# Where the low halves of a product's operands are made: a subtraction on VectorE, or a negated copy on ScalarE and an adding transfer

## The chip, the cores and the metric

One core of a Trainium2 chip runs the whole kernel in one launch. The metric is the device time of one execution in microseconds, the median over runs. TensorE does the matrix products, VectorE (DVE), ScalarE (ACT) and GpSimd (POOL) the elementwise work, and transfers are issued by SyncE (SP) and GpSimd.

## The reference

One layer of a decoder trunk with 512 tokens of 1024 channels, in float32. Two gated token mixers (a convolution and a chunked linear attention) are merged and projected; then comes the channel mixer, which the change touches, and a last normalization:

```python
merged = jax.nn.sigmoid(gate_a) * y_conv + jax.nn.sigmoid(gate_b) * y_gla
h = h + merged @ w_o[l]

u2 = _rmsnorm(h, norm2_g[l])
z = _causal_dwconv(u2 @ w_ffn_up[l], ffn_dw_w[l], ffn_dw_b[l])      # 2 x 2816 channels, width 3
h = h + (jax.nn.silu(z[..., :FFN_DIM]) * z[..., FFN_DIM:]) @ w_ffn_down[l]
...
return _rmsnorm(h, final_g)
```

## The kernel before

A float32 product is made of three TensorE products of a rounded format (float32r). Each operand x is split in a high part, hi = x rounded, and a low part, lo = x - hi; `mm3` (lines 448 to 450) then issues low times high, high times low, and high times high into the same accumulator. The left operand of a matmul is loaded as the weights, the right one streams by. So each operand needs a rounding copy (on ScalarE) and a subtraction (on VectorE), and a matmul can't start before both parts of both operands are there. For weights, `split_weight` does it (lines 355 and 356, and 385 and 390); for the sixteen weight tiles in `ADDED`, line 387 writes the negated copy with ScalarE and line 388 adds the weight to it by a transfer from off-chip memory that GpSimd issues.

The channel mixer has 22 tiles of 128 channels. They are handled in pairs, and the pairs in three groups of four, three and four (`GROUPS`). For each group the up products of its tiles come first, in an order that `up_plan` gives; the up products are `col_tile` for single tiles and `two_tiles` for two at once, whose summed weights GpSimd makes (line 327). A tile's two accumulators are convolved (lines 1500 and 1503), passed through silu (1511) and multiplied (1517). The result of the first tile of a pair is `w`, that of the second is `f`. When a group's up products are done, `seven("w_down", ...)` makes the group's part of the down product for 1024 output channels, and adds it to the residual `hres` (line 1419).

`seven` does a product of two by two blocks by seven block products instead of eight. For each pair of tiles, it needs seven left operands: blocks of `w` and `f`, and sums of such blocks. They are made in three steps, each of them ending in `fsplit`, which makes the high and the low part of one tile:

- `first_of_pair`: `w` gets a third block (line 1533); tile y (`yh`, `yl`, 512 columns) holds the operands named a11 and n3.
- `second_of_pair`: tile a (`ah`, `al`, 512 columns) holds a12 and a22, from `f`.
- `second_of_pair`, further on: three sums of blocks into `v` (lines 1543 to 1545); tile s (`sh`, `sl`, 768 columns) holds s1, n2 and s4.

With 11 pairs, that is 33 calls of `fsplit`. The split tiles have four buffers each; `w`, `f` and `v` have one. The products within `seven` go by steps: a11 for the pairs first, then a12, s1 and the others, each with two pairs at a time, so TensorE reads yl first, then al, then sl. For the down weights, `sum_on` (line 317) and the line 300 add further blocks of the weight to a loaded one by transfers that GpSimd issues.

The order of the instructions on each engine is that of the recording, changed by a scheduler; transfers and weight sums that are kept in program order, and constraints of the form "issue after", hold it in places. Transfers that GpSimd issues go to one queue, and a place on GpSimd's instruction stream comes when all before it have been issued.

Of the kernel before, what the change touches and what calls it, by code (L numbers as in the profile page):

```python
# [10 lines left out]
F32 = mybir.dt.float32  # L11
# [4 lines left out]
ALU = mybir.AluOpType  # L16
# [3 lines left out]
T = 512  # L20
# [55 lines left out]
def trunk_layer(ctx: ExitStack, tc: tile.TileContext, a: dict, out: bass.AP):  # L76
    nc = tc.nc
# [23 lines left out]
    def nm(s):  # L101
        return f"{s}_{next(names)}"

    def heap(dt=F32):
        return hp.tile([P, T], dt, tag="h", name=nm("h"))
# [710 lines left out]
    for k in range(KT):  # L816
# [4 lines left out]
        c = heap()  # L821
# [108 lines left out]
    for k in range(KT):  # L930
        s = slice(k * P, (k + 1) * P)
# [49 lines left out]
    class Head:  # L981
# [99 lines left out]
        def gated(self, last=False):  # L1081
            for s in range(2):
                po = ax_bank() if s or last else mm_bank()
                for p in range(NT):
                    nc.tensor.transpose(po[:, p * P : (p + 1) * P], self.o[:, p, s * P : (s + 1) * P], ident)  # L1085
                f = tmp()
                m = 2 * self.h + s
                nc.vector.scalar_tensor_tensor(f, po, pp[:, PP_GG + s : PP_GG + s + 1], sr[m], ALU.mult, ALU.mult)
                oa[m] = split(f)
# [14 lines left out]
    H = T // 2  # L1104
# [404 lines left out]
    def value(i, acc):  # L1509
        za = ffn_conv(acc, i)  # L1510
        nc.scalar.activation(za, za, AF.Silu)
        return za
# [3 lines left out]
        zb = ffn_conv(acc, FT + i)  # L1516
        nc.vector.tensor_tensor(out, za, zb, ALU.mult)

    def fsplit(src, n, tag):
        hi, lo = (fp.tile([P, n], F32R, tag=tag + p, name=nm(tag + p), bufs=4) for p in "hl")  # L1520
        shaped = (lambda x: x.rearrange("p (c t) -> p c t", t=H)) if len(src.shape) == 3 else (lambda x: x)
        nc.scalar.copy(shaped(hi), src)
        nc.vector.tensor_tensor(shaped(lo), src, shaped(hi).bitcast(F32), ALU.subtract)
        return lambda c, n=1: tuple(x[:, c * H : (c + n) * H] for x in (hi, lo))

    def first_gated(i, za, acc):
        w = fp.tile([P, 3 * H], F32, tag="w", name=nm("w"), bufs=1)
        gated(i, za, acc, w[:, :T])
        return w

    def first_of_pair(w):

        nc.vector.tensor_tensor(w[:, T:], w[:, :H], w[:, H:T], ALU.subtract)
        y = fsplit(w.rearrange("p (c t) -> p c t", t=H)[:, 0:3:2, :], T, "y")
        return {"a11": y(0), "n3": y(1)}

    def second_of_pair(i, za, acc, w, acts):

        f = fp.tile([P, T], F32, tag="f", name=nm("f"), bufs=1)
        gated(i, za, acc, f)  # L1540
        v = fp.tile([P, 3 * H], F32, tag="v", name=nm("v"), bufs=1)
        s1, n2, s4 = (v[:, c * H : (c + 1) * H] for c in range(3))
        nc.vector.tensor_tensor(s1, w[:, H:T], f[:, H:], ALU.subtract)
        nc.vector.tensor_tensor(n2, s1, w[:, :H], ALU.subtract)
        nc.vector.tensor_tensor(s4, f[:, :H], n2, ALU.add)
        y = fsplit(f, T, "a")
        acts["a12"], acts["a22"] = y(0), y(1)
        y = fsplit(v, 3 * H, "s")
        acts["s1"], acts["n2"], acts["s4"] = y(0), y(1), y(2)
        return acts  # L1550

# [76 lines left out]
    for gi, pairs in enumerate(GROUPS):  # L1628
        acts = []
        if gi == 0:  # L1630

            ws = [weight("w_up", j, 0) for i in pairs[0] for j in (i, FT + i)]
            accs = [mm_bank() for _ in ws]
            for j, lo in [(j, lo) for lo in (0, H) for j in range(3)]:
                late = {(1, 0): (KT - 1, 2), (2, 0): (MID, 3)}.get((j, lo))
                at = {late[0]: lambda t=late[1]: to_channels(normed[t], u2, t)} if late else {}
                col_tile(ws[j], acts2, accs[j], lo, lo + H, at)
            col_tile(ws[3], acts2, accs[3])
            p, q = pairs[0]
            w = first_gated(p, value(p, accs[0]), accs[1])  # L1640
            found = first_of_pair(w)
            up_acts, sums = ffn_sums()
            s1_n2, of_s1, s4, of_n2, of_s4, n3, of_n3 = sums
            sums = [s1_n2, of_n2 + of_s1, s4 + n3, of_n3 + of_s4]

            def some_sums():
                for _, work in sums.pop(0) if sums else ():
                    work()

            some_sums()  # L1650
            acts.append(second_of_pair(q, value(q, accs[2]), accs[3], w, found))
            some_sums()
        else:
            found = first_of_pair(w)
        for what, i, *rest in up_plan(gi):
            if what == "tile":
                if 0 in rest[0]:
                    banks[i] = (weight("w_up", i), mm_bank())
                wt, acc = banks[i]
                col_tile(wt, acts2, acc, ks=rest[0])  # L1660
                if KT - 1 in rest[0] and i < FT:
                    values[i] = value(i, acc)
            if what == "part":
                if rest[0] == "x1":
                    units[i] = two_tiles("w_up", i, FT + i, lambda: up_acts, ax_bank)
                done = next(units[i])
                if done:
                    values[i] = value(i, done[0])
                    banks[FT + i] = (None, done[1])
                    third = [taps_at[0], third_ahead()]  # L1670
            if what == "first":
                w = first_gated(i, values.pop(i), banks.pop(FT + i)[1])
                if any(i in pair for pair in pairs):
                    found = first_of_pair(w)
            if what == "second":
                with ExitStack() as order_of:
                    for ins in third:
                        if ins:
                            order_of.enter_context(tc.issue_after(ins.ins))
                    acts.append(second_of_pair(i, values.pop(i), banks.pop(FT + i)[1], w, found))  # L1680
                third = []
            if what in ("first", "second"):
                some_sums()
# [95 lines left out]
```

## Time and profile before

| | |
|---|---|
| Median of three runs | 821.08 us (821.05 to 822.15) |
| The profiled execution: its time | 820.78 us |
| Its span, first to last instruction | 818.9 us |
| Mean granted TensorE clock | 0.999 |
| DMA traffic | 106.25 MB, mean 130 GB/s |
| `fsplit`'s subtractions (line 1523) | 33, from 495 to 784 us of the span |

The page of the profile gives each engine's busy time and its share of the span, the granted clock by slices, the DMA queues, the chain of work that ended last, the groups of instructions by line, and the DMA issues with their size and the time from issue to landing. A timeline row gives the start within the span, the duration, the engine, the line, the operation, what is written and read, and, in brackets, how long the engine had been idle and what released it. In a group's row stand the busy time and the mean time of one in ns.

### The profile page before, as it was taken

Reading aid. Unit: us, or ns where it says so; the run is one execution under the profiler, and the core shown is the slowest. Engines: PE = TensorE matmul, PEld = TensorE weight load, DVE = VectorE, ACT = ScalarE, POOL = GpSimd, SP = SyncE. Lnnn points to the kernel's source line nnn. Section 1 sums busy time; section 2 is a strip of 40 time slices with the busy share of each in tenths; the row PEclk is TensorE's granted clock in tenths of the full one; section 3 lists DMA queues with packets and bytes.
Section 4 is the critical chain, followed back from the end, with each engine's and each line's share of the span. In section 5 each row is a group of like instructions: output and inputs, shape, how many; then the busy total and the mean of one; then the engine's idle time right before and its main releaser. Section 6 shows DMA issues by size and latency. Waiting matters only on the chain.

```text
span 818.9 us, 11480 instructions
## 1 busy us (share of the span) xinstructions
PE 810.3 (99%) x4287; PEld 700.5 (86%) x4287; DVE 715.6 (87%) x1157; ACT 448.9 (55%) x666; POOL 148.8 (18%) x133
## 2 busy tenths in 40 slices
PE   9999999999999999999999999999999999999996
PEld 7888888888888889999988898898889988899885
DVE  6689999999989699885788889979965999789896
ACT  6643447656663446684444556556435663466554
POOL 2000010001000213633001000230123301622012
PEclk9999999999999999999999999999999999999999
DMA  8355572563532123223657623146642447334662
GB/s 318 104 127 144 148 188 96 130 154 104 120 97 96 49 62 109 88 78 129 206 115 220 187 71 103 52 161 166 134 137 89 144 123 167 104 103 177 158 129 102
DMA packets 30615, 106.25 MB, mean 130 GB/s; under 512 B 3464, under 2 KB 3600, under 8 KB 30560
## 3 DMA queue, kind: packets, MB, share of 16 engines
q1 hardware_dynamic: 24784, 85.34, 30.4%
q0 software_dynamic: 5760, 20.19, 14.4%
q8 instruction: 33, 0.54, 0.3%
q14 instruction: 22, 0.18, 0.1%
q10 hardware_dynamic: 16, 0.00, 0.0%
HBM read 103.42 MB, written 2.10 MB: 129 GB/s over the span
## 4 chain that ended last, share of the span: by engine, by line
PE 98%; DMA 1%; ACT 0%; DVE 0%; POOL 0%; issue 0%; POOLq 0%; SPq 0%; ACTq 0%
PE mm L448 28%; PE mm L449 28%; PE mm L450 28%; PE mm L662 3%; PE ax L450 2%; PE ax L448 2%; PE ax L449 2%; PE ax L1070 1%; PE ax L1072 1%; PE ax L1051 1%; DMA raw<-in_w_v_dram 1%; PE ax L1040 0%; PE ax L529 0%; PE ax L576 0%; PE ax L1085 0%; PE mm L933 0%
## 5 line engine op out<-in xcount | busy, mean ns | idle before, releaser
L448 PE MATMUL mm<-uh,wlo 128*128 128x512 f32 (+1 forms) x672 | 244.4, 364 | 0.0
L449 PE MATMUL mm<-ul,whi 128*128 128x512 f32 (+1 forms) x672 | 242.4, 361 | 0.0
L450 PE MATMUL mm<-uh,whi 128*128 128x512 f32 (+1 forms) x672 | 242.0, 360 | 0.0
L450 PEld LDWEIGHTS mm<-uh,whi 128*128 128x128 f32 x672 | 126.8, 189 | 19.4
L448 PEld LDWEIGHTS mm<-uh,wlo 128*128 128x128 f32 x672 | 127.0, 189 | 18.8
L449 PEld LDWEIGHTS mm<-ul,whi 128*128 128x128 f32 x672 | 127.0, 189 | 18.6
L385 ACT CAST whi<-raw 128x1024 fp32r<-128x1024 f32 x86 | 89.7, 1047 | 54.9 <-PE mm L450 28.2
L356 DVE TENSOR_TENSOR wlo<-raw,whi 128x1024 fp32r<-128x1024 f32 x80 | 93.1, 1171 | 24.4 <-ACT whi L355 20.5
L327 POOL TENSOR_TENSOR raw<-raw,raw 128x512 f32<-128x512 f32 x42 | 67.6, 1610 | 212.8 <-DVE wlo L356 130.7
L390 DVE TENSOR_TENSOR wlo<-raw,whi 128x1024 fp32r<-128x1024 f32 x70 | 92.7, 1327 | 14.1 <-ACT whi L385 14.0
L355 ACT CAST whi<-raw 128x1024 fp32r<-128x1024 f32 x80 | 76.3, 957 | 34.8 <-PE mm L450 27.2
L788 DVE SCALAR_TENSOR_TENSOR c<-h,pp,c 128x255 f32<-128x255 f32 (+14 forms) x120 | 57.5, 479 | 4.0 <-ACT c L784 3.7
L788 DVE SCALAR_TENSOR_TENSOR c<-aside,btmp,c 128x255 f32<-128x255 f32 (+14 forms) x120 | 57.5, 479 | 1.4 <-ACT c L784 1.4
L788 DVE SCALAR_TENSOR_TENSOR aside<-h,pp,aside 128x255 f32<-128x255 f32 (+6 forms) x112 | 53.7, 479 | 0.0
L355 ACT CAST whi<-kept 128x1024 fp32r<-128x1024 f32 (+1 forms) x32 | 31.8, 996 | 31.8 <-DVE kept L310 17.0
L1503 DVE SCALAR_TENSOR_TENSOR tmp<-mm,pp,tmp 128x511 f32<-128x511 f32 (+1 forms) x56 | 41.4, 742 | 4.0 <-ACT tmp L1500 3.9
L356 DVE TENSOR_TENSOR wlo<-kept,whi 128x1024 fp32r<-128x1024 f32 (+1 forms) x32 | 36.8, 1153 | 4.8 <-ACT whi L355 4.7
L1181 ACT COPY tmp<-mm 128x256 f32<-128x256 f32 x48 | 17.7, 368 | 34.4 <-PE mm L450 34.0
L1419 DVE TENSOR_TENSOR hres<-hres,mm 128x512 f32<-128x512 f32 (+1 forms) x49 | 32.3, 671 | 4.7 <-PE mm L450 3.4
L1500 ACT ACTIVATE tmp<-mm,pp 128x512 f32<-128x512 f32 x28 | 21.8, 779 | 19.0 <-PE mm L450 18.9
L387 ACT ACTIVATE wlo<-raw 128x1024 fp32r<-128x1024 f32 x16 | 16.9, 1060 | 22.1 <-PE mm L448 22.1
L1503 DVE SCALAR_TENSOR_TENSOR tmp<-tmp,pp,tmp 128x511 f32<-128x511 f32 (+1 forms) x32 | 27.8, 887 | 0.4
(347 smaller groups left out, 1767.0 us busy)
## 6 DMA issues: line engine op xcount, KB each, us to landing
raw<-in_w_up_dram SPq DMA_DIRECT2D x44, 512.0 KB, 3.5
raw<-in_w_glu_dram SPq DMA_DIRECT2D x16, 512.0 KB, 5.2
raw<-in_w_down_dram SPq DMA_DIRECT2D x15, 512.0 KB, 4.3
kept<-in_w_down_dram POOLq DMA_DIRECT2D x10, 512.0 KB, 5.9
raw<-in_w_v_dram SPq DMA_DIRECT2D x8, 512.0 KB, 5.6
raw<-in_w_qk_dram SPq DMA_DIRECT2D x8, 512.0 KB, 3.4
raw<-in_w_r_dram SPq DMA_DIRECT2D x8, 512.0 KB, 4.6
wlo<-in_w_r_dram POOLq DMA_DIRECT2D x8, 512.0 KB, 8.1
```

What stands on the lines that cost most here:

```text
L327: work = nc.gpsimd.tensor_tensor(out, x, y, ALU.add)
L355: nc.scalar.copy(hi, raw)
L356: two_low[:] = [nc.vector.tensor_tensor(lo, raw, hi.bitcast(F32), ALU.subtract)]
L385: nc.scalar.copy(hi, raw)
L390: pace[0] = nc.vector.tensor_tensor(lo, raw, hi.bitcast(F32), ALU.subtract)
L448: nc.tensor.matmul(acc, ll, rh, start=first, stop=False, **kw)
L449: nc.tensor.matmul(acc, lh, rl, start=False, stop=False, **kw)
L450: nc.tensor.matmul(acc, lh, rh, start=False, stop=last, **kw)
L662: nc.tensor.matmul(acc, act, ready[k // 2][wi][:, j], start=first, stop=last)
L788: nc.vector.scalar_tensor_tensor(out[:, j:], x[:, : half_t - j], w, out[:, j:], ALU.mult, ALU.add)
L1419: done = nc.vector.tensor_tensor(hres[t, n][:, c], hres[t, n][:, c], acc[:, c], op)
L1503: nc.vector.scalar_tensor_tensor(z[:, s:], acc[:, : T - s], w[j], z[:, s:], ALU.mult, ALU.add)
```

## The change

In `fsplit` the low part of all three kinds of tiles is made in another way. ScalarE writes the negated copy of the source, rounded by the format of `lo`, to `lo`, and a transfer issued by GpSimd, from the source's place in the on-chip memory to `lo`, adds the source to it. As `lo` holds the float32r-rounded negative, the sum is the low part. VectorE has no part in it any more.

```diff
-    def fsplit(src, n, tag):
+    def fsplit(src, n, tag, added=False):
         hi, lo = (fp.tile([P, n], F32R, tag=tag + p, name=nm(tag + p), bufs=4) for p in "hl")
         shaped = (lambda x: x.rearrange("p (c t) -> p c t", t=H)) if len(src.shape) == 3 else (lambda x: x)
         nc.scalar.copy(shaped(hi), src)
-        nc.vector.tensor_tensor(shaped(lo), src, shaped(hi).bitcast(F32), ALU.subtract)
+        if added:
+            nc.scalar.mul(shaped(lo), src, -1.0)
+            nc.gpsimd.dma_start(shaped(lo), src, accum_op=ALU.add)
+        else:
+            nc.vector.tensor_tensor(shaped(lo), src, shaped(hi).bitcast(F32), ALU.subtract)
         return lambda c, n=1: tuple(x[:, c * H : (c + n) * H] for x in (hi, lo))
...
-        y = fsplit(w.rearrange("p (c t) -> p c t", t=H)[:, 0:3:2, :], T, "y")
+        y = fsplit(w.rearrange("p (c t) -> p c t", t=H)[:, 0:3:2, :], T, "y", True)
...
-        y = fsplit(f, T, "a")
+        y = fsplit(f, T, "a", True)
         acts["a12"], acts["a22"] = y(0), y(1)
-        y = fsplit(v, 3 * H, "s")
+        y = fsplit(v, 3 * H, "s", True)
```

## The prediction

> **What bounds the kernel now.** I read the page's busy shares first, then its chain of work that ended last, then the waits of TensorE, then single stretches of the timeline.
>
> ```profile
> PE 810.3 (99%) x4287; PEld 700.5 (86%) x4287; DVE 715.6 (87%) x1157; ACT 448.9 (55%) x666; POOL 148.8 (18%) x133
> ...
> PE 98%; DMA 1%; ACT 0%; DVE 0%; POOL 0%; issue 0%; POOLq 0%; SPq 0%; ACTq 0%
> PE mm L568 <- DVE ones L541: 1.1, 1, 1.1
> PE mm L662 <- ACT h L589: 0.8, 1, 0.8
> ...
> 811.97 0.28 PE L450 MATMUL mm<-whi,ah 128*128 128x256 f32 x1
> ```
>
> TensorE carries 98% of the chain. Its whole list of waits is these two, 1.9 us, both in the kernel's opening, far from the feed-forward part that the change touches. The last matmul starts at 811.97 of a span of 818.9. Two things follow. A lighter VectorE (87% busy) can't shorten the time, since TensorE waits for it nowhere behind the opening: the gain side is empty. And an operand that comes late to TensorE is paid in full, as nothing later has slack to give back. So the question is how late, and for which matmuls, the new low parts come.
>
> **What is removed, and by what it is replaced.**
>
> ```profile
> L1523 DVE TENSOR_TENSOR sl<-v,sh 128x768 fp32r<-128x768 f32 x11 | 10.4, 948 | 0.0
> L1523 DVE TENSOR_TENSOR yl<-w,yh 128x512 fp32r<-128x512 f32 x11 | 8.7, 790 | 0.8 <-ACT yh L1522 0.6
> L1523 DVE TENSOR_TENSOR al<-f,ah 128x512 fp32r<-128x512 f32 x11 | 7.5, 681 | 0.0
> L300 POOL DMA_DIRECT2D raw<-in_w_down_dram x6 | 5.2, 860 | 44.9 <-DVE hres L1419 23.3 <-DVE kept L310 7.5 <-DVE al L1523 7.3
> ```
>
> 33 subtractions, 10.4 + 8.7 + 7.5 = 26.6 us, leave VectorE; worth nothing by the above, except where they let another operand come sooner. Added are 33 negated copies on ScalarE, which I price as the casts of the same tiles (0.62 and 0.83 us in the timeline below; some 23 us on an engine 55% busy), and 33 transfers issued by GpSimd at 0.86 us each, 28 us on an engine 18% busy. Per tile, 0.7 to 0.9 us between the cast and the matmul becomes: copy 0.6 to 0.8, a place in GpSimd's order, then the landing. Landings are in the list of DMA issues (KB each, median us from issue to landing):
>
> ```profile
> raw<-in_w_down_dram POOLq DMA_DIRECT2D x5, 512.0 KB, 5.5
> ...
> raw<-in_w_down_dram SPq DMA_DIRECT2D x3, 256.0 KB, 2.6
> ...
> kept<-in_w_down_dram POOLq DMA_DIRECT2D x2, 256.0 KB, 7.1
> ...
> raw<-in_w_down_dram POOLq DMA_DIRECT2D x1, 256.0 KB, 3.9
> ...
> 684.29 0.85 POOL L317 DMA_DIRECT2D kept<-in_w_down_dram  x1 [0.33 <-issue]
> 685.49 0.88 POOL L317 DMA_DIRECT2D kept<-in_w_down_dram  x1 [0.35 <-DVE wlo L356]
> ```
>
> GpSimd's rows here are all adding transfers, from off-chip memory. Alone, 512 KB took 5.5 us and 256 KB 3.9: 1.6 us for each 256 KB on 2.3 fixed. The x2 row is two small ones behind bigger ones: 7.1. Back to back, issues start 1.2 us apart. No row has the on-chip memory as the source. So yl and al (256 KB) take 3.9 if alone and sl (384 KB) 4.7; behind another they take 1.6 and 2.4 more than it (my value: the queue is worked off in order); the bad end is the 7.1. The good end for something this new is the plain transfer's 2.6, which I keep as a rival.
>
> [...]
>
> In the built order of the changed kernel TensorE's and SyncE's instructions stand as before but for one exchanged matmul, and GpSimd's 33 issues stand among its accumulating weight loads (L300, L317) and weight sums (L327). The low parts of most pairs wait for TensorE to finish the up products; only those of the last pair of each of the three groups are read soon after they are made.
>
> **Last group (4.7 us).** In the last pair of group 2 VectorE works without a gap:
>
> ```profile
> 769.08 0.68 DVE L1523 TENSOR_TENSOR al<-f,ah 128x512 fp32r<-128x512 f32 x1
> 769.68 0.41 DVE L1544 TENSOR_TENSOR v<-v,w 128x256 f32<-128x256 f32 x1
> ...
> 772.27 0.95 DVE L1523 TENSOR_TENSOR sl<-v,sh 128x768 fp32r<-128x768 f32 x1
> 773.14 0.42 DVE L1533 TENSOR_TENSOR w<-w 128x256 f32<-128x256 f32 x1
> ...
> 774.61 0.68 DVE L1523 TENSOR_TENSOR yl<-w,yh 128x512 fp32r<-128x512 f32 x1
> ...
> 771.13 0.83 ACT L1522 CAST sh<-v 128x768 fp32r<-128x768 f32 x1 [0.80 <-DVE v L1545]
> 772.45 0.64 ACT L1511 ACTIVATE tmp<-tmp 128x512 f32<-128x512 f32 x1 [0.49 <-DVE tmp L1503]
> 773.59 0.62 ACT L1522 CAST yh<-w 128x512 fp32r<-128x512 f32 x1 [0.51 <-DVE w L1533]
> ...
> 769.48 0.86 POOL L317 DMA_DIRECT2D kept<-in_w_down_dram  x1 [5.19 <-ACT tmp L1500]
> ...
> 775.89 0.39 PE L448 MATMUL mm<-whi,yl 128*128 128x512 f32 x1
> ...
> 785.41 0.39 PE L448 MATMUL ax<-whi,al 128*128 128x512 f32 x1
> ...
> 788.13 0.39 PE L448 MATMUL mm<-whi,sl 128*128 128x512 f32 x1
> ```
>
> Before, yl is ready at 774.61 + 0.68 = 775.3 and read at 775.89: 0.6 us in hand. Without al's 0.60 and sl's 0.87 (start to start), w's last step ends not at 773.56 but at 772.1. ScalarE by then: sh from about 770.65 to 771.5, sl's copy to 772.2, the activation of L1511 to 772.75, yh to 773.3, yl's copy to 773.85. GpSimd: L317 at 769.48 (landing 775.0 by 5.5), al at about 770.7, sl at 772.5, yl at 774.1. In order al lands at 776.6, sl at 779.0, yl at 780.6: 4.7 us after 775.89. If the queue didn't matter, yl lands at 774.1 + 3.9 = 778.0: 2.1. At the bad end al takes 7.1 to 777.8, then 2.4 and 1.6 make 781.8: 5.9. The last pair's al and sl are read from 785.41 and 788.13 on, which this stall moves back by 4.7: room for their copies and landings, so nothing for them.
>
> **Group 1 (2.7 us).**
>
> ```profile
> 675.35 0.86 POOL L300 DMA_DIRECT2D raw<-in_w_down_dram  x1 [7.27 <-DVE al L1523]
> ...
> 674.77 0.84 ACT L1522 CAST sh<-v 128x768 fp32r<-128x768 f32 x1 [1.05 <-DVE v L1545]
> ...
> 680.80 0.39 PE L448 MATMUL ax<-whi,al 128*128 128x512 f32 x1
> ...
> 682.16 0.39 PE L448 MATMUL mm<-whi,sl 128*128 128x512 f32 x1
> ```
>
> The two rows of TensorE are the first that read the last pair's al and sl. In the changed order the L300 stands ahead of al and sl; it lands by 675.35 + 5.5 = 680.85. al, issued at 676.6, lands 1.6 later, 682.45: 1.65 late. sl's copy is done by 676.4, its issue at 677.8, its landing 2.4 after al's, 684.85, where TensorE now wants it at 683.81: 1.04 more. Together 2.7. Without queueing 676.6 + 3.9 is in time and sl, 677.8 + 4.7 = 682.5, is 0.3 late. At the bad end al lands at 683.7, sl at 686.1: 2.9 + 1.0 = 3.9.
>
> **Group 0 (0.5 us).**
>
> ```profile
> 575.08 0.84 POOL L300 DMA_DIRECT2D raw<-in_w_down_dram  x1 [6.80 <-DVE v L1545]
> ...
> 581.72 0.39 PE L448 MATMUL ax<-whi,al 128*128 128x512 f32 x1
> ...
> 584.44 0.39 PE L448 MATMUL mm<-whi,sl 128*128 128x512 f32 x1
> ```
>
> Again the L300 stands ahead, landing by 580.6; al, issued at 576.3, lands at 582.2, 0.5 late; sl at 584.6, within that. Without queueing nothing is late (580.2, 582.3); at the bad end al lands at 583.4: 1.7.
>
> **The body (0).** Where the weight sums of GpSimd stand behind the new issues, one place is tight:
>
> ```profile
> L356 DVE TENSOR_TENSOR wlo<-raw,whi 128x1024 fp32r<-128x1024 f32 x80 | 93.1, 1171 | 24.4 <-ACT whi L355 20.5 <-PE mm L450 3.7
> ...
> L355 ACT CAST whi<-raw 128x1024 fp32r<-128x1024 f32 x80 | 76.3, 957 | 34.8 <-PE mm L450 27.2 <-POOL raw L327 3.7 <-PE ax L450 2.2
> ...
> 526.76 0.41 DVE L1545 TENSOR_TENSOR v<-f,v 128x256 f32<-128x256 f32 x1
> ...
> 518.04 3.01 POOL L327 TENSOR_TENSOR raw<-raw,raw 128x512 f32<-128x512 f32 x2 [41.40 <-DVE wlo L390]
> ...
> 534.43 0.28 PE L448 MATMUL mm<-xq,wlo 128*128 128x256 f32 x1
> ```
>
> Sums that began at 518.04 now stand behind sl's issue. With VectorE left as it is, v ends at 527.2, cast and copy at 528.9, the issue at 529.8, two sums (3.0) at 532.8, then the summed weight's cast and its low part (0.96 and 1.17) at 534.9, 0.5 behind the matmul at 534.43. But a yl's and an al's subtraction ahead of v are gone (790 and 681 ns), so it just fits: 0, at the bad end 0.5. A transfer's wait for the one eight before it falls on landings long past, and a next write to w, f or v waits for a landing that is over by then.
>
> **Sum.** 4.7 + 2.7 + 0.5 = 7.9 us. Against the profiled execution's 820.78 (span 818.9, the rest around it unchanged; the median of the runs is 821.08, 0.3 away): 828.7. Both ends: 2.1 + 0.3 + 0 = 2.4 gives 823.2; 5.9 + 3.9 + 1.7 = 11.5 gives 832.3.
>
> **Rivals.** *Hidden*: the adding transfer from on-chip memory lands like the plain 256 KB, 2.6 us after its issue, and nothing ahead holds it. Then groups 0 and 1 are in time (676.6 + 2.6 = 679.2 against 680.80) and yl in group 2 lands at 776.7: 0.8 late, 821.6, not slower by what can be measured (some 0.2%, 1.6 us, is what this kernel's runs can tell from no change). [...] Against: every adding row is slower. It decides if yl's landing stays under 3.4 us (775.89 + 1.6 - 774.1).
>
> *Heavier queue*: small transfers behind big ones go as the 7.1 row: 832.3.
>
> *The clock.* Behind the last matmul the granted clock (PEclk, third from the right) falls:
>
> ```profile
> 814.00:819.00 5.00, 0.00 (x0) 0.00 (x0) 0.55 (x1) 0.61 (x1) 0.30 (x1) 0.79 0.37 152
> ```
>
> If it is full and then half, a mean of 0.79 puts the drop at 816.9, 4.7 us after the last matmul's end at about 812.2. My stall of 4.7 us is at that point. If it drops and stays half as long as it took to fall, 2.35 us more are lost: 831.0.
>
> [...]
>
> *Body*: the shifted weight sums come late in more places than the one priced, at 0.5 each; three of them give 830.2. Against: GpSimd is idle for most of the span.
>
> *Faster*: only if VectorE had been holding TensorE; the waits say no, and I find no more than the 0.3 us between profile and median.
>
> **How the numbers follow.** Forecast 828.7: 0.50. Hidden 821.6: 0.08. Heavier queue 832.3: 0.17. Clock 831.0: 0.15. Body 830.2: 0.08. Faster: 0.02. The range takes in the forecast's low end (823.2, a little lower for a part-hidden transfer: 822.4), the heavy queue, and some of the clock's price on top of it: 833.5. Faster 0.02, same 0.08, slower the rest, 0.90.
>
> **What would show it.** Right: three new waits of TensorE for low parts that a DMA releases, about 4.7 us before the first yl of group 2's last pair, about 1.7 and 1.0 at group 1's last al and sl, under 1 in group 0; new landings from 4 to 7 us; 26.6 us less of VectorE's busy time. Wrong: landings under 3 us, TensorE with no new wait, a wait in the middle of a group, or a granted clock below full around 776 to 785.

## The result, and the profile after

The changed kernel takes 843.13 us (median of four runs, 840.43 to 847.18) against 821.07 before: a ratio of 1.0269, 95% interval 1.0248 to 1.0290. That is 22 us slower; 7.6 us were forecast, and the range ended at 833.5. The profiled execution took 842.09 us, with a span of 840.4.

The page after: busy times, and two lines from its list of DMA issues (KB, median us to landing); the last two lines are from the full list of transfers.

```profile
span 840.4 us, 11591 instructions
PE 816.8 (97%) x4287; PEld 702.7 (84%) x4287; DVE 694.6 (83%) x1124; ACT 467.5 (56%) x699; POOL 182.1 (22%) x166
...
kept<-in_w_down_dram POOLq DMA_DIRECT2D x10, 512.0 KB, 7.6
sl<-v POOLq DMA_DIRECT2D x11, 384.0 KB, 5.8
...
yl<-w POOLq DMA_DIRECT2D x11, 256.0 KB, 5.1
al<-f POOLq DMA_DIRECT2D x11, 256.0 KB, 6.2
```

VectorE is 21 us lighter and TensorE 6.5 us "busier", though it issues the same matmuls; 3.7 us of that are matmuls that ran at a lower clock. The waits of TensorE say where the rest went (releaser, us in total, times, longest):

```profile
PE mm L448 <- DMA yl<-w: 4.6, 1, 4.6
PE mm L448 <- DVE hres L1419: 4.5, 1, 4.5
PE ax L448 <- ACT tmp L1181: 3.4, 3, 1.6
PE ax L448 <- DMA al<-f: 1.6, 1, 1.6
...
PE mm L448 <- ACT tmp L1181: 0.5, 1, 0.5
PE mm L448 <- DMA sl<-v: 0.3, 1, 0.3
```

Only the lines that name a DMA are waits for a low part. I measure a stall as the time between two starts of matmuls beyond the usual 0.227 us (0.121 for 256 columns); it comes out a little larger than the waits. By that measure the profiled execution lost 7.3 us to late low parts (0.2 in group 0, 1.7 and 0.5 in group 1, 4.8 in group 2), 4.7 to a stall that ended at 706.5, 3.8 to three evictions by ScalarE (0.4, 1.8 and 1.7; L1181: a copy that empties an accumulator bank, `ax`, for the next product), 0.6 to one more eviction (of an `mm` bank, at 656.8), and 3.7 in slow matmuls behind the two long stalls. That is 20.1 of the 21.5 us by which the last matmul moved, from 811.97 to 833.45.

The two long stalls, and the granted clock behind them (windows: us; busy of PE, PEld, DVE, ACT, POOL; then PEclk):

```profile
706.51 0.76 PE L448 MATMUL mm<-whi,al 128*128 128x512 f32 x1 [4.53 <-DVE hres L1419]
796.01 0.53 PE L448 MATMUL mm<-whi,yl 128*128 128x512 f32 x1 [4.63 <-DMA yl<-w]
```

```profile
704.00:706.00 2.00, 0.00 (x0) 0.00 (x0) 1.72 (x2) 2.00 (x3) 2.00 (x2) 0.55 0.00 0
...
796.00:800.00 4.00, 3.99 (x11) 3.12 (x12) 2.49 (x4) 1.29 (x2) 0.24 (x1) 0.57 0.81 130
800.00:804.00 4.00, 4.00 (x19) 3.33 (x18) 3.31 (x5) 3.87 (x6) 1.21 (x2) 1.00 0.42 75
```

In 4 us behind the second stall 11 matmuls went out, in the next four 19. The stall at 706.51 ended with a `hres` update (L1419), which empties an accumulator. The products before the stall had ended by about 702.0; the update came at 705.70, since on VectorE it stood behind the low part of a weight (L356), and that behind the weight's cast:

```profile
703.63 0.62 ACT L355 CAST whi<-kept 128x512 fp32r<-128x512 f32 x1 [5.32 <-DMA kept<-in_w_down_dram]
...
704.28 1.49 DVE L356 TENSOR_TENSOR wlo<-kept,whi 128x512 fp32r<-128x512 f32 x1 [4.51 <-ACT whi L355]
705.70 1.27 DVE L1419 TENSOR_TENSOR hres<-hres,mm 128x512 f32<-128x512 f32 x2
```

The cast waited for the landing of a weight addition. GpSimd's timeline shows the weight additions of group 1 (L317) with group 2's first yl between them:

```profile
688.82 0.85 POOL L300 DMA_DIRECT2D raw<-in_w_down_dram  x1 [7.53 <-DVE hres L1419]
689.39 1.18 POOL L317 DMA_DIRECT2D kept<-in_w_down_dram  x1
692.87 1.20 POOL L1525 DMA_DIRECT2D yl<-w  x1 [2.30 <-issue]
697.40 0.90 POOL L317 DMA_DIRECT2D kept<-in_w_down_dram  x1 [3.33 <-DVE hres L1419]
```

Before, the two additions went out 1.2 us apart; here the second goes out 8 us behind the first and takes 6.1 us to land (703.5). Only then can its weight be cast, its low part be made, and the update behind it run. The products that waited are the first ones with a22 (I call this the stall at a22).

There is a pattern in such starts. A transfer that GpSimd issues is 144 packets, but yl's is 272 (two 1 KB pieces a partition; 11,920 packets on the queue against 5,760 before). Counting what is in flight at each start, there are at most 432 packets in this trace. In 12 places the next transfer would have made 560 or 576, and each of those starts 0.31 to 0.33 us behind an earlier landing. Three theories followed: GpSimd's queue holds transfers back for want of room; the order in it decides; ScalarE's two added copies come ahead of evictions.

### The profile page after: what moved, and what is told of

It reads as the page before. It is cut to its first block, busy times and chain, and to the rows that moved or that the text cites. A ratio compares the mean times of both kernels' runs of the same rounds, so it can differ in the third digit from the quotient of the medians.

```text
span 840.4 us, 11591 instructions
## 1 busy us (share of the span) xinstructions
PE 816.8 (97%) x4287; PEld 702.7 (84%) x4287; DVE 694.6 (83%) x1124; ACT 467.5 (56%) x699; POOL 182.1 (22%) x166
## 3 DMA queue, kind: packets, MB, share of 16 engines
q0 software_dynamic: 11920, 30.28, 20.7%
## 5 line engine op out<-in xcount | busy, mean ns | idle before, releaser
L356 DVE TENSOR_TENSOR wlo<-raw,whi 128x1024 fp32r<-128x1024 f32 x80 | 97.4, 1221 | 31.9 <-ACT whi L355 27.8
L327 POOL TENSOR_TENSOR raw<-raw,raw 128x512 f32<-128x512 f32 x42 | 69.5, 1656 | 134.5 <-DVE wlo L356 93.2
L1503 DVE SCALAR_TENSOR_TENSOR tmp<-mm,pp,tmp 128x511 f32<-128x511 f32 (+1 forms) x56 | 41.7, 744 | 10.9 <-ACT tmp L1500 10.5
L356 DVE TENSOR_TENSOR wlo<-kept,whi 128x1024 fp32r<-128x1024 f32 (+1 forms) x32 | 37.7, 1178 | 12.4 <-ACT whi L355 12.3
L1419 DVE TENSOR_TENSOR hres<-hres,mm 128x512 f32<-128x512 f32 (+1 forms) x49 | 32.6, 672 | 12.8 <-PE mm L450 12.7
L1181 ACT COPY tmp<-mm 128x256 f32<-128x256 f32 x48 | 17.6, 366 | 33.1 <-PE mm L450 32.5
L388 POOL DMA_DIRECT2D wlo<-in_w_r_dram x8 | 7.0, 879 | 97.8 <-ACT junk L1074 32.4
```

The lines of the kernel that those rows point to most:

```text
L327: work = nc.gpsimd.tensor_tensor(out, x, y, ALU.add)
L356: two_low[:] = [nc.vector.tensor_tensor(lo, raw, hi.bitcast(F32), ALU.subtract)]
L1419: done = nc.vector.tensor_tensor(hres[t, n][:, c], hres[t, n][:, c], acc[:, c], op)
L1503: nc.vector.scalar_tensor_tensor(z[:, s:], acc[:, : T - s], w[j], z[:, s:], ALU.mult, ALU.add)
```

## The experiments

**Room in the queue.** `y_contig`: the blocks of `w` are put in the order n3, first half, second half.

```diff
...
-        nc.vector.tensor_tensor(w[:, T:], w[:, :H], w[:, H:T], ALU.subtract)
-        y = fsplit(w.rearrange("p (c t) -> p c t", t=H)[:, 0:3:2, :], T, "y", True)
-        return {"a11": y(0), "n3": y(1)}
+        nc.vector.tensor_tensor(w[:, :H], w[:, H:T], w[:, T:], ALU.subtract)
+        y = fsplit(w[:, :T], T, "y", True)
+        return {"a11": y(1), "n3": y(0)}
...
```

> The three blocks of w change places (n3 first, then the product's two halves), so that yl's transfer has one contiguous piece of 2 KB a partition instead of two of 1 KB; nothing else changes, nor the order of any engine. Theory (room in GpSimd's queue): a yl transfer is 272 packets, the others 144; GpSimd holds a transfer back while more than some 432 to 560 packets would be in flight, so with 144 for yl its waits for an earlier landing (starts 0.31 to 0.33 us behind one) go, and so does the 4.7 us stall at group 1's a22 with the slow clock behind it (6.9 us): about 834 us. Rival (landing times): the transfers are simply slow and in order, whatever their pieces: 841 to 843, the a22 stall stays.

Measured: 841.64 us, ratio 1.0258 (1.0239 to 1.0277). The holding back went as the theory has it; the time didn't. GpSimd's rows of the same yl, first of the changed kernel, then of this one:

```profile
642.87 0.84 POOL L1525 DMA_DIRECT2D sl<-v  x1 [3.13 <-ACT sl L1524]
645.31 1.21 POOL L1525 DMA_DIRECT2D yl<-w  x1 [1.60 <-ACT whi L355]
```

```profile
645.41 0.85 POOL L1525 DMA_DIRECT2D sl<-v  x1 [3.14 <-ACT sl L1524]
646.51 0.86 POOL L1525 DMA_DIRECT2D yl<-w  x1 [0.25 <-issue]
...
693.56 0.86 POOL L317 DMA_DIRECT2D kept<-in_w_down_dram  x1 [1.68 <-DVE hres L1419]
```

2.4 us behind sl there, 1.1 here. The only starts 0.31 us behind a landing are now the three where a fourth transfer of 144 would make 576; the last row is one. That L317 goes out 3.8 us earlier than in the changed kernel, but takes 11.0 us to land instead of 6.1, with yl still ahead of it and three loads beside it, and the stall at a22 stays (5.2 us in the waits). So these starts went with the packets, but starts that come sooner brought no time.

`a_split`: on top of that, `f` gets a gap between its halves, so that al has two pieces.

```diff
...
+        f = fp.tile([P, 3 * H], F32, tag="f", name=nm("f"), bufs=1)
+        f2 = f.rearrange("p (c t) -> p c t", t=H)[:, 0:3:2, :]
+        gated(i, za, acc, f2)
...
+        y = fsplit(f2, T, "a", True)
...
```

> With w's blocks contiguous as in the first run, f gets a gap between its two halves, so that al's transfer has the two 1 KB pieces (272 packets) that yl's had. Theory (room in GpSimd's queue): the held-back starts, 0.31 to 0.33 us behind a landing, come back, now also for sl and for loads behind al; group 1's sl starts behind the landing of the load two before it; about 838 us. Rival (something peculiar to yl and its place, not the packets): no held-back starts, the same time as the first run within 1 us.

838.01 us, ratio 1.0209 (1.0192 to 1.0226). The held-back starts are back, 12 of them at 560 or 576, among them sl behind al, which never was held before. They went with the packets here too, not with something about yl. The total fell as forecast, but the stall at a22 isn't there, and why it isn't is not shown. With 12 held-back starts this kernel is faster than `y_contig` with three, so their number doesn't set the time.

**Who makes the copy.** `neg_dve`:

```diff
-            nc.scalar.mul(shaped(lo), src, -1.0)
+            nc.vector.tensor_scalar(shaped(lo), src, -1.0, None, ALU.mult)
```

> The negated copy is made by VectorE, not by ScalarE; the transfers stay. Theory (ScalarE's order): the stalls of 0.4, 1.8 and 1.7 us at the first matmul into an ax bank late in a group come from the copies of sl and yl ahead of that bank's eviction on ScalarE, and go: about 838 us, the 4.7 and 4.8 us stalls stay. Rival (GpSimd's queue delays all of it): 841 to 843, the three stalls stay.

833.16 us, ratio 1.0156 (1.0136 to 1.0176): 5 us better than expected. The three waits for L1181 are gone, but so is the one at a22. The edit let the scheduler put group 2's first yl behind both weight additions, so it changes two things and separates nothing. `contig_neg_dve` adds the contiguous blocks.

> Both edits together. If the two causes are separate, their gains add: about 830 us, with group 1's al and sl stalls (2.2 us) and group 2's yl stall (about 4.5 us and 1.5 of slow clock behind it) left. If one of them hides the other, no better than the better one alone.

834.40 us, ratio 1.0173 (1.0151 to 1.0195): no gain from room on top. The sum of gains that I had put at 830 wasn't there.

**One exchange.** `yl_behind` undoes just that: on GpSimd, the yl transfer goes behind the second weight addition.

```diff
...
-            found = first_of_pair(w)
+            with tc.issue_after(kept['last'].ins): found = first_of_pair(w)
```

> One exchange on GpSimd against the changed kernel: group 2's first yl transfer is issued behind the second of group 1's last two weight additions (L317), not between them; TensorE, VectorE and ScalarE keep their orders. Theory (place in the queue): the weight addition lands some 4 us earlier, the 4.7 us stall at group 1's a22 and the 2.1 us of slow clock behind it go: about 836 us, all other stalls as they were. Rival (the weight addition is late since the DMA engines are full of other loads): the stall keeps over 3 us, 840 or more.

839.85 us, ratio 1.0230 (1.0206 to 1.0254). The weight additions go out together again, and the stall at a22 is gone: the one wait that TensorE has left under the name of `hres` is far ahead of the channel mixer.

```profile
690.25 0.85 POOL L300 DMA_DIRECT2D raw<-in_w_down_dram  x1 [7.31 <-DVE wlo L356]
690.82 2.06 POOL L317 DMA_DIRECT2D kept<-in_w_down_dram  x2
698.52 1.20 POOL L1525 DMA_DIRECT2D yl<-w  x1 [5.64 <-issue]
```

```profile
465.84 0.47 PE L448 MATMUL mm<-whi,h 128*128 128x512 f32 x1 [1.05 <-DVE hres L1419]
```

The stalls of its profiled execution add to 15.1 us against 20.3. The median moved by half of what I expected, and its interval overlaps the changed kernel's (1.0248 to 1.0290): that the stall goes is shown by the profile, not by the time. The runs of these kernels spread by 3 to 7 us. With so many transfers close to their due time, each execution may be late somewhere else; that isn't shown.

`evict_first` calls `first_of_pair` when the next unit's third product begins, so that ScalarE has the eviction ahead of yh and yl.

```diff
+                if rest[0] == "x2" and "w" in kept: found = first_of_pair(kept.pop("w"))
...
-                    found = first_of_pair(w)
+                    kept["w"] = w
...
```

> First_of_pair is called later in the recording, so that three times ScalarE evicts an ax bank (L1181) ahead of yh and yl's copy instead of behind them; TensorE's order is unchanged. Theory (ScalarE's order): the stalls of 0.4, 1.8 and 1.7 us at the first matmul into those banks go: about 839 us; the stall at a22 and those at al, sl and yl stay. Rival (the waits are GpSimd's): they stay, 842 to 843.

841.42 us, ratio 1.0256 (1.0222 to 1.0291): inconclusive by time. ScalarE's rows at the same place, changed kernel first:

```profile
662.88 0.84 ACT L1524 ACTIVATE sl<-v 128x768 fp32r<-128x768 f32 x1
663.62 0.60 ACT L1522 CAST yh<-w 128x512 fp32r<-128x512 f32 x1
664.13 0.62 ACT L1524 ACTIVATE yl<-w 128x512 fp32r<-128x512 f32 x1
664.66 0.35 ACT L1181 COPY tmp<-ax 128x256 f32<-128x256 f32 x1
```

```profile
667.93 0.84 ACT L1524 ACTIVATE sl<-v 128x768 fp32r<-128x768 f32 x1
668.68 0.35 ACT L1181 COPY tmp<-ax 128x256 f32<-128x256 f32 x1
```

And from its waits of TensorE:

```profile
PE ax L448 <- DMA al<-f: 5.0, 1, 5.0
...
PE ax L448 <- ACT tmp L1181: 0.4, 2, 0.3
```

The wait for L1181 falls from 3.4 to 0.4 us, as the theory has it. But this execution, at 846.5 us the slowest of the four, also waited 5.0 us for group 0's last al, which was in time in the changed kernel's. Both edits together (`behind_and_evict`) settle it better.

> Both edits together. If the two causes are separate, 6.8 and 3.8 us go: about 832 us. What is left are the waits for the last pairs' own transfers, some 2.5 us in groups 0 and 1 and 6.4 at group 2's yl with its slow clock.

835.32 us, ratio 1.0170 (1.0154 to 1.0186): 0.0099 below the changed kernel's ratio, some 8 us, against the 11 expected. Left in its profile are 2.8 us for al and sl in group 1, 0.8 for sl in group 0, 0.6 at an eviction, and 7.8 at yl with its slow clock.

**What makes the low parts late.** `al_ahead`, on the last: L300 is issued behind al and sl.

```diff
...
-            nc.gpsimd.dma_start(dst, block(name, pairs, d, 1, 1), accum_op=ALU.add)
+            with tc.issue_after(kept["lo"].ins) if "lo" in kept else ExitStack(): nc.gpsimd.dma_start(dst, block(name, pairs, d, 1, 1), accum_op=ALU.add)
...
```

> On behind_and_evict: GpSimd issues the last pairs' al and sl ahead of the weight load (L300) that stood before them; nothing else moves on any engine. Theory (order of the queue): al and sl of groups 0 and 1 land 1.5 to 2.5 us sooner, the 3.6 us of stalls there fall to under 1: about 832.5 us, with group 2's yl left. Rival (the landing is their own, some 6 us whatever is ahead): no change from 835.3.

The landing of group 1's last al, in the changed kernel and here, by the tile's view:

```profile
DMA to landing us min/median/max: 6.6/6.6/6.6
```

```profile
DMA to landing us min/median/max: 3.3/3.3/3.3
```

The waits of TensorE in `al_ahead` name no al and no sl any more, but:

```profile
PE mm L448 <- DVE hres L1419: 5.3, 1, 5.3
PE mm L448 <- DMA yl<-w: 4.7, 1, 4.7
```

With no L300 ahead, al takes 3.3 us, and sl 3.9 instead of 7.6: the rival falls. The run moved one thing more, though. In the changed kernel a load of SyncE's started 2.5 us behind this al and was in flight until al had landed; here al had landed before it started. Such loads count too. In the changed kernel eight als went out with nothing ahead on GpSimd's queue: two took 3.2 and 3.6 us (issued at 504.4 and 525.3), and the six with a load of SyncE's started beside them, within 1.7 us of their issue, took 4.5 to 6.5.

The time is 840.08 us, ratio 1.0207 (1.0190 to 1.0223), 3 us worse by the ratios: now the L300 lands at 687.3, the second L300 starts later, the two L317 land 10 and 11 us behind their issue, and the a22 products wait 5.3 us. The wait changed hands.

`contig_behind_evict` asks whether the want of room makes group 2's yl late.

> On behind_and_evict: w's blocks contiguous, so that yl's transfer is 144 packets and isn't held back on GpSimd for want of room; no engine's order changes. Theory (what counts is the queue's order, al and sl ahead of yl): yl of group 2's last pair is issued 1 to 2.5 us sooner but lands no sooner than 1.6 us behind sl, so within 0.5 us of the same time: 835 us of the same runs before, that is a ratio of 1.017. Rival (the holding back is what makes yl late): the 7.8 us at that yl fall to 3 or so, a ratio of 1.011.

The chain of waits at that yl, `behind_and_evict` first ("issue" is the time that it wasn't sent; POOLq is GpSimd's sequencer):

```profile
777.72 0.85 POOL sl L1525
778.58 3.00 issue
...
781.59 4.97 DMA yl<-w
```

```profile
783.95 0.83 POOL sl L1525
784.78 1.66 issue
...
786.45 5.81 DMA yl<-w
792.31 0.79 PE mm L448
```

Against sl it is sent 1.3 us sooner, and takes 0.8 longer. It lands 1.3 us behind sl; that was 1.9. Against what I expected, this start is still a held one: it comes 0.31 us behind the landing of an L317 (786.1), where a fourth transfer of 144 packets would have made 576. So the run shortens the holding back and doesn't remove it. The stall with its slow clock is 7.1 us where it was 7.8: 1.3 us of holding back were worth 0.7, and what the rest costs stays open. The total is 838.24 us, ratio 1.0198 (1.0179 to 1.0216), higher than I expected, since TensorE waited 5.5 us for al in groups 0 and 1: in group 1 the L300 ahead of al waited for its own block, which landed at 681.1, beside two weight additions.

**One tile kind at a time.** `as_dve` transfers only yl, `y_dve` only al and sl:

```diff
 as_dve
-        y = fsplit(f, T, "a", True)
+        y = fsplit(f, T, "a")
-        y = fsplit(v, 3 * H, "s", True)
+        y = fsplit(v, 3 * H, "s")
 y_dve
-        y = fsplit(w.rearrange("p (c t) -> p c t", t=H)[:, 0:3:2, :], T, "y", True)
+        y = fsplit(w.rearrange("p (c t) -> p c t", t=H)[:, 0:3:2, :], T, "y")
```

> The opposite: only yl (11 of the 33) by transfer, al and sl by VectorE's subtraction. Theory: only group 2's yl stalls; with no al and sl ahead of it in the queue it lands about 3.7 us after an issue at about 776.2 of before's clock: 3.5 to 4.5 us late and at the edge of the slow clock, 825 to 827 us. Rival (what holds yl is al and sl ahead of it): at most 2 us late, 823.

826.14 us, where the kernel before took 823.03 beside it: ratio 1.0036 (1.0022 to 1.0051). By the time both forecasts fit (as ratios to 821.07, 1.0048 to 1.0072 and 1.0024). One stall of 1.6 us is left at that yl: with al and sl out of its way it lands 4.1 us behind its issue. So the rival was right, that al and sl hold it; and no lower clock follows the stall: the mean granted clock of its profiled execution is 0.999, as before.

> yl by VectorE's subtraction again, al and sl (22 of the 33) by transfers; TensorE's order unchanged. Theory: the stall at group 2's yl (4.8 us and 1.6 of slow clock), the one at a22 (4.7 and 2.1) and every held-back start on GpSimd go (no more than 432 packets in flight); the last pairs' al and sl in groups 0 and 1 (about 2.5 us) and a part of ScalarE's late bank evictions (some 2 us) stay: about 826 us. Rival (the transfers' number is what costs, a third fewer save a third): 836.

832.34 us, ratio 1.0117 (1.0102 to 1.0132), more than I thought. One held-back start is left (796.8), where I expected none. The largest of its waits:

```profile
PE ax L448 <- DMA al<-f: 6.0, 3, 3.9
```

The 3.9 us are the last al of group 2, which I had priced at nothing because it stood behind yl's stall. With that stall gone it is the next that is late, and the slow clock comes with it (1.5 us).

**All of the last pairs.** `last_pairs_dve` has both edits of `behind_and_evict`, and seven of 33 low parts by VectorE again.

```diff
...
+    LAST = {("y", 10)} | {(t, n) for t in "as" for n in (3, 6, 10)}
...
-        if added:
+        kept[tag] = kept.get(tag, -1) + 1
+        if added and (tag, kept[tag]) not in LAST:
...
```

> Both edits, and the low parts of the last pairs (al and sl in all three groups, yl in group 2: seven of 33) by VectorE's subtraction again. Theory: the rest of the loss goes with them, 821 to 822.5 us, not faster than before since TensorE had no wait to save. Rival (26 transfers on GpSimd's queue still cost by themselves, in issue time or in the loads beside them): 824 or more.

823.76 us, ratio 1.0031 (1.0017 to 1.0044). In its profiled execution (822.22 us) only 0.7 us of stalls are left:

```profile
PE 812.4 (99%) x4287; PEld 701.3 (85%) x4287; DVE 691.9 (84%) x1131; ACT 462.9 (56%) x692; POOL 172.2 (21%) x159
```

```profile
PE ax L448 <- ACT tmp L1181: 0.2, 1, 0.2
```

With 26 transfers VectorE is 23.7 us lighter than before, and it brings nothing. The median is still 1.4 to 3.6 us above before. Why its other executions are longer than the profiled one isn't shown.

## Why the prediction was wrong

What bounds the kernel, and that a lighter VectorE is worth nothing, held: no kernel here was faster than before.

The terms of the sum came out near: group 2 4.8 us (4.7 forecast), group 1 2.25 (2.7), group 0 0.2 (0.5), 7.3 in all against 7.9. That a low part lands later for what stands ahead of it in the queue, `al_ahead` bears out, though a load of SyncE's was out of the way there too. That the sizes agree is in part luck. Group 2's yl was to go out 1.8 us before TensorE wanted it and to take 6.5; it went out just when TensorE wanted it (791.18), 0.33 behind al's landing, and took 4.8. Group 1's al went out 0.8 us sooner, measured against its due time, and took 6.6 where I had 5.85. The single price, 3.9 for 256 KB and 4.7 for 384 KB, stood for two cases: 3.2 to 3.6 and 3.8 to 4.0 with little or nothing ahead or beside, and for al 4.5 to 6.5 with loads of SyncE's beside it, which I didn't price.

**The step that failed is "The body (0)"**, where everything but the last pairs' own low parts was put at nothing. The sentence before the groups, that only the last pairs' low parts are read soon, held: every low part that came late in the profile after is one of a last pair. But I followed the 33 new transfers to their own readers, and not each thing that they were put ahead of.

- GpSimd's order had a yl between group 1's two L317. I priced L300 ahead of al, not yl ahead of L317. The second weight came late, on VectorE a `hres` update stood behind its low part, and TensorE waited 4.7 us; `yl_behind` takes that away by one exchange.
- ScalarE's copies were priced as time on an engine 55% busy. They went ahead of evictions that TensorE waited for: 3.8 us; `evict_first` takes most of those waits away.
- In the body I looked at one place, the weight sums. There the profile after shows no stall. Another eviction (656.8) cost 0.6 us; on ScalarE it stood behind an activation that waited for VectorE's convolution (L1503), and why that came late isn't shown.

With both edits and the last pairs' low parts made by VectorE, `last_pairs_dve` is within 0.3% of before, where the changed kernel was 2.7% above: the body's two terms and the late low parts, with the clock behind them, hold nearly all of the loss.

Two of the signs that I had named for being wrong are there: waits in the middle of a group, and a granted clock below full, behind that same yl.

**The rivals** were each priced as if the others didn't happen. The clock's did: 2.1 and 1.6 us behind the two long stalls, where I had 2.35 for one. With the body's 4.7 + 3.8 + 0.6, that is 12.8 us on top of the forecast terms, and the range had room for 4.8. That the clock stays at half for as long as it took to fall was my estimate, and the trace doesn't bear it out. Behind the first stall it fell 2.6 us after the last matmul had begun and was half for 6.83 us, 4.5 of them with TensorE busy; behind the second it fell 5.35 us after and was half for 3.42 us, with TensorE busy throughout. *Body* fell as it was meant: no wait of TensorE's in the profile after ends with a weight sum. *Hidden* fell: none of the 33 transfers landed in less than 3.2 us, and the late ones took 4.8 to 7.6. *Heavier queue*, too, by its terms: 1.7, 3.9 and 5.9 us against 0.2, 2.25 and 4.8.

Group 2's other operands, put at nothing behind the stall, are worth nothing only there (`y_dve`: 3.9 us).

## What to carry to other kernels

When a transfer joins a queue, price it for everything issued behind it and for the loads beside it, not only for its own reader; and price an added copy by what is behind it on its engine, not by the engine's share. A late operand that one edit cures can hand its wait to the next one, so count what each stall was hiding. Rivals that can happen together belong in the range as a sum.

## What the runs showed of the hardware

- In the changed kernel's trace GpSimd's queue had at most 432 packets in flight. Twelve transfers that would have made 560 or 576 were sent 0.31 to 0.33 us behind the next landing. That a want of room holds them back is my reading of the counts and the starts. Splitting a 256 KB transfer in 1 KB pieces made 272 packets of 144 (yl: 11,920 packets on the queue in the changed kernel, 10,512 in `y_contig`, where it is in one piece a partition).
- An adding transfer within the on-chip memory took 3.2 to 3.6 us (al, 256 KB: 3.2 and 3.6 in the changed kernel, 3.3 in `al_ahead`) and 3.8 to 4.0 (sl, 384 KB: 3.8 and 4.0 in the changed kernel, 3.9 in `al_ahead`) with little or nothing ahead or beside, and up to 9.9 in the changed kernel (yl, issued at 770.98) behind others and beside loads of SyncE's.
- The granted clock of the changed kernel fell behind both long stalls, and not equally long after the last matmul. In the first stall it was 1.00 up to 704.18 (mean 0.55 over 704 to 706): it fell 2.6 us after the last matmul had begun (701.60), and was 0.50 from there to 711.01. In the second it was still 1.00 4.5 us after (790.99; 1.00 up to 795.5). It fell at 796.34, when the matmuls had resumed (796.01), and was 0.50 to 799.76. Below are the 3.41 us ahead of the first fall, and the two such stretches ahead of the second (length; busy of PE, PEld, DVE, ACT, POOL; then PEclk). The clock is 0.50 behind the first and the third, and 1.00 behind the second. What decides when it falls isn't shown.

```profile
700.77:704.18 3.41, 1.22 (x6) 0.68 (x4) 0.00 (x0) 0.55 (x2) 1.48 (x2) 1.00 0.57 132
789.51:792.93 3.42, 1.86 (x9) 1.21 (x7) 3.23 (x4) 0.90 (x1) 1.19 (x1) 1.00 1.08 252
792.93:796.34 3.41, 0.33 (x1) 0.30 (x2) 0.00 (x0) 0.00 (x0) 0.91 (x1) 1.00 0.65 133
```
